# Splitting 24 weight tiles during the first feed-forward, and token-major last down products, in a hybrid decoder layer

## The chip, the cores and the metric

The kernel runs on one core of one Trainium2 chip. The metric is the time of one execution on the device, in microseconds, median of several runs. The engines named below are PE (TensorE, matrix products; PEld is its weight load), DVE (VectorE), ACT (ScalarE), POOL (GpSimd) and SP (SyncE, which here only issues DMAs).

## The reference, cut to what matters

One decoder layer over 1032 tokens: a prompt of 1024 and 8 sample tokens that each have a paged cache of 2048. All arrays are fp32, the model width is 1024, the feed-forward width 2816.

```python
def swiglu(x, wg, wu, wd):
    return (jax.nn.silu(x @ wg) * (x @ wu)) @ wd
...
h = layer_norm(ALPHA * x + 0.5 * swiglu(x, ffn1_wg, ffn1_wu, ffn1_wd), ln1_g, ln1_b)
q_a, k_a, v_a, q_i, k_i, w_i, q_r, k_r, v_r, g_r = jnp.split(h @ w_in, _split_points(), axis=-1)
o_a = attend(q_a, k_a, v_a, q_i, k_i, w_i)   # indexer scores, top-k keys per query, softmax over them
o_r, s_new = retention(qr, kr, vr, s0)       # 4 heads of 128, chunkwise, with rotary q and k
mix = jnp.concatenate([o_a.reshape(B, S, W_A), y_r], axis=-1) @ w_out
h = layer_norm(ALPHA * h + mix, ln2_g, ln2_b)
h = layer_norm(ALPHA * h + 0.5 * swiglu(h, ffn2_wg, ffn2_wu, ffn2_wd), ln3_g, ln3_b)
```

Outputs are the last h for prompt and sample, the new keys, values and indexer keys, and the retention states.

## The kernel before, in words

**Tiling and precision.** Activations lie feature-major: 128 features on the partitions, tokens along the row, in three chunks of 344 tokens (CW). Each fp32 product is made of three matmuls (`mm3`, lines 169 to 171): an operand is split into a high part (a rounded copy) and a low part (the remainder), and high by high, high by low and low by high are added up in PSUM. A weight tile is 128 x 1024, 512 KB.

**Stages.** First feed-forward (0 to about 745 us): chunk 0 by plain products, then chunks 1 and 2 together (`chunks12`) by products of a seven-product scheme, over eleven pairs p of feed-forward tiles; the down products of pairs 9 and 10 come last (`last`). Then the first layer norm, the projections with `w_in` (chunk-wise products named pw_qi, pw_kr and so on), indexer scores (around 800 to 890), the top-k search beside the retention heads (890 to 1110), ties, attention (1150 to 1340), the output projection with `w_out` (1340 to 1470), the sample tokens' attention, and the second feed-forward (about 1520 to 2290). At its end the output's layer norm (`ln_out`) follows on the last down products.

**The weight tiles of the middle.** `Weights` holds a list of tiles in the order of use. `w_raw` has SP load one tile into a single raw buffer (line 142); `w_split` has ACT cast it to the high part (line 152) and GpSimd subtract for the low part (line 154), into one of two pairs of buffers. While one pair is in use by a product, the next tile is split into the other pair as soon as its last reader is done, and the next raw load follows. The list is: three indexer query tiles (qi1 to qi3), gr0, then kr, vr, qr and gr of heads 1 to 3, then the twelve tiles va, qa and ka of attention, then the eight tiles wo of the output projection, and ten more.

**Order.** The program is written as generators that a scheduler (`g.s`) steps by a modelled time: a `yield` of so many microseconds or `tick` moves it. The order in which instructions stand on each engine follows from that, and each engine works its own list in order. The feed-forward's weights stream through a free list of slots (`g.fs`); `Stream.keep` is the number of slots that the stream leaves free.

**The tail.** `f2.last(c, after)` makes, for each of 8 output tiles o of 128 features, 12 matmuls of 344 tokens (weights stationary, lines 403 to 405), then VectorE adds the result to z (line 407). `ln_out` makes for each tile of 128, 128 or 88 tokens eight transposes back to token-major (line 710), statistics (lines 713 and 716), the reciprocal root (lines 633 to 638), two scalings and additions per half of 512 features (line 720, then 722 on ACT and 723 on GpSimd, or 725 on VectorE), and an output DMA (lines 727 and 729).

## Time and profile before

| | us |
|---|---|
| median of 3 runs | 2312.18 |
| lowest and highest run | 2311.66, 2313.08 |
| the profiled execution | 2311.91 |
| its span in the trace | 2310.1 |

The profiled execution is one run; its span is the time from the first to the last instruction that the trace holds. A row of a timeline reads: start, duration, engine, line, operation, output<-inputs, shapes, and in brackets the idle time before it with what ended it. "The chain of waits" is followed back from the last instruction, at each step to what released it. Names of tiles are those of the program: wr_ is a raw weight tile, wh_ and wl_ its high and low parts, pw_ a projection's PSUM tile, zt the small tables of the search.

### The profile page before, as it was taken

The page shows a single profiled execution, that of the slowest core. Times are in us where ns is not written, and L with a number is a line of the kernel's source. Part 1 is how long each engine was busy: PE and PEld are TensorE (multiplying, and loading weights), DVE is VectorE, ACT ScalarE, POOL GpSimd, SP SyncE. Part 2 cuts the span into 40 slices and gives each one's busy share as a digit, 9 for nine tenths or more (in the row PEclk, how much of TensorE's full clock was granted, in tenths as well). Part 3 has the DMA queues.
Part 4 walks back from the last instruction along what each step waited for, and adds up shares of the span by engine and source line. Part 5 has one row for each costly group of instructions (what it writes and reads, how often), then busy time and mean ns, then how long its engine had stood idle before and what let it go on. Part 6 is the DMA issues. An engine that isn't in the chain of part 4 may idle for free.

```text
span 2310.1 us, 36886 instructions
## 1 busy us (share of the span) xinstructions
PE 2220.8 (96%) x14155; PEld 2144.3 (93%) x14155; DVE 1761.8 (76%) x3745; ACT 1072.4 (46%) x1931; POOL 323.4 (14%) x342
## 2 busy tenths in 40 slices
PE   8999999999999999889899999889999999999996
PEld 8999999999999989778789989879799999999996
DVE  5655797887878578678966678988568789887866
ACT  5433343332334465878466665343435444333331
POOL 0000100000002303444122234313210000000002
PEclk9999999999999999999999999989999999999998
DMA  8544332222222211121332142336544332222211
GB/s 266 156 136 146 109 89 74 83 75 64 82 75 97 93 25 46 53 69 49 88 89 56 51 141 80 121 123 189 177 129 137 98 103 80 92 73 65 92 65 49
DMA packets 239182, 224.32 MB, mean 97 GB/s; under 512 B 13098, under 2 KB 219774, under 8 KB 238238
## 3 DMA queue, kind: packets, MB, share of 16 engines
q1 hardware_dynamic: 235166, 209.38, 30.0%
q0 software_dynamic: 3840, 12.59, 1.7%
q8 instruction: 111, 1.82, 0.3%
q14 instruction: 65, 0.53, 0.1%
HBM read 200.91 MB, written 22.59 MB: 97 GB/s over the span
## 4 chain that ended last, share of the span: by engine, by line
PE 78%; DVE 11%; ACT 6%; issue 3%; DMA 1%; POOL 0%; POOLq 0%; SPq 0%; DVEq 0%; ACTq 0%
PE pds_f L403 5%; PE pds_f L404 5%; PE pds_f L405 5%; PE pg_f L169 2%; PE pu_f L169 2%; PE pg_f L170 2%; PE pg_f L171 2%; PE pdp_f L403 2%; PE pu_f L171 2%; PE pu_f L170 2%; PE pdp_f L404 2%; PE pdp_f L405 2%; ACT ja L1034 2%; PE ps_f1U L169 2%; PE ps_f2G L170 2%
## 5 line engine op out<-in xcount | busy, mean ns | idle before, releaser
L407 DVE SCALAR_TENSOR_TENSOR z<-pds_f,z 128x344 f32<-128x344 f32 x320 | 164.6, 516 | 125.9 <-PE pds_f L405 124.7
L403 PE MATMUL pds_f<-gs_f,wh_f1ds 128*128 128x344 f32 x352 | 114.1, 325 | 0.1
L407 DVE SCALAR_TENSOR_TENSOR z<-pdp_f,z 128x344 f32<-128x344 f32 x160 | 80.0, 512 | 44.1 <-PE pdp_f L405 43.9
L403 PE MATMUL pds_f<-gs_f,wh_f2ds 128*128 128x344 f32 x352 | 113.4, 322 | 0.0
L405 PE MATMUL pds_f<-gs_f,wl_f1ds 128*128 128x344 f32 x352 | 113.2, 322 | 0.0
L404 PE MATMUL pds_f<-gs_f,wh_f1ds 128*128 128x344 f32 x352 | 113.1, 321 | 0.0
L405 PE MATMUL pds_f<-gs_f,wl_f2ds 128*128 128x344 f32 x352 | 112.4, 319 | 0.0
L404 PE MATMUL pds_f<-gs_f,wh_f2ds 128*128 128x344 f32 x352 | 112.4, 319 | 0.0
L1034 ACT ACTIVATE ja<-key,zt 128x1024 bf16<-128x1024 int16 (+5 forms) x90 | 93.7, 1041 | 34.6 <-DVE zt L1045 33.1
L723 POOL TENSOR_TENSOR yt<-yt,ln_b_rows 128x512 f32<-128x512 f32 (+1 forms) x9 | 12.0, 1352 | 570.3 <-ACT yt L722 570.3
L296 ACT CAST wS_f1G<-ws_f1G 128x512 fp32r<-128x512 f32 x44 | 25.0, 618 | 133.5 <-PE pds_f L404 68.1
L1508 ACT CAST p<-pT 128x512 fp32r<-128x512 f32 (+2 forms) x112 | 47.4, 433 | 54.1 <-PE pT L1504 41.9
L296 ACT CAST wS_f2G<-ws_f2G 128x512 fp32r<-128x512 f32 x44 | 25.7, 619 | 93.4 <-PE pds_f L405 80.7
L403 PEld LDWEIGHTS pds_f<-gs_f,wh_f1ds 128*128 128x128 f32 x352 | 66.8, 190 | 1.1 <-DVE z L407 0.3
L404 PEld LDWEIGHTS pds_f<-gs_f,wh_f1ds 128*128 128x128 f32 x352 | 66.7, 190 | 0.2
L405 PEld LDWEIGHTS pds_f<-gs_f,wl_f1ds 128*128 128x128 f32 x352 | 66.7, 189 | 0.0
L403 PEld LDWEIGHTS pds_f<-gs_f,wh_f2ds 128*128 128x128 f32 x352 | 66.2, 188 | 0.2 <-ACT gs_f L465 0.2
L404 PEld LDWEIGHTS pds_f<-gs_f,wh_f2ds 128*128 128x128 f32 x352 | 66.2, 188 | 0.0
L405 PEld LDWEIGHTS pds_f<-gs_f,wl_f2ds 128*128 128x128 f32 x352 | 66.1, 188 | 0.0
L612 POOL TENSOR_TENSOR lns_l<-z 128x344 f32<-128x344 f32 x3 | 2.8, 929 | 442.2 <-DVE z L407 428.0
L1509 DVE TENSOR_TENSOR p<-pT,p 128x512 fp32r<-128x512 f32 (+2 forms) x112 | 54.5, 497 | 8.7 <-ACT p L1508 7.5
L1470 ACT ACTIVATE z<-z,mn 128x896 f32<-128x896 f32 (+3 forms) x64 | 49.8, 778 | 20.0 <-DVE mn L1467 15.7
(815 smaller groups left out, 8651.0 us busy)
## 6 DMA issues: line engine op xcount, KB each, us to landing
wr_f1g<-in_ffn_wg_dram SPq DMA_DIRECT2D x22, 512.0 KB
wr_f1u<-in_ffn_wu_dram SPq DMA_DIRECT2D x22, 512.0 KB
wr_f1dp<-in_ffn_wd_dram SPq DMA_DIRECT2D x22, 512.0 KB
wr_f1G<-in_ffn_wg_dram SPq DMA_DIRECT2D x22, 512.0 KB
wr_f1U<-in_ffn_wu_dram SPq DMA_DIRECT2D x22, 512.0 KB
wr_f1ds<-in_ffn_wd_dram SPq DMA_DIRECT2D x22, 512.0 KB
wr_f2u<-in_ffn_wu_dram SPq DMA_DIRECT2D x22, 512.0 KB
wr_f2g<-in_ffn_wg_dram SPq DMA_DIRECT2D x22, 512.0 KB
```

The source lines that it names most:

```text
L169: g.nc.tensor.matmul(ps, w[0][:, k, :], x[0][:, k, :], start=first and i == 0, stop=False)
L170: g.nc.tensor.matmul(ps, w[0][:, k, :], x[1][:, k, :], start=False, stop=False)
L171: g.nc.tensor.matmul(ps, w[1][:, k, :], x[0][:, k, :], start=False, stop=last and i == n - 1)
L296: nc.scalar.copy(t[:, 0], src)
L403: g.nc.tensor.matmul(ps, wh[:, o, :], th, start=i == 0, stop=False)
L404: g.nc.tensor.matmul(ps, wh[:, o, :], tl, start=False, stop=False)
L405: g.nc.tensor.matmul(ps, wl[:, o, :], th, start=False, stop=i == len(grp) - 1)
L407: g.nc.vector.scalar_tensor_tensor(out=z, in0=ps, scalar=0.5 / ALPHA, in1=z, op0=OP.mult, op1=OP.add)
L1034: nc.scalar.activation(jk[:, 0:n], key[b], AF.Sign, bias=t[:, j:j + 1], scale=-1.0, accum_out=cnt[:, j:j + 1])
L1470: nc.scalar.activation(z[:, 0:n], z[:, 0:n], AF.Exp, bias=prev, scale=-1.0, accum_out=mn[:, 3:4])
L1508: nc.scalar.copy(ph[:, js, ts], ptv[:, js, ts])
L1509: nc.vector.tensor_tensor(out=pl[:, js, ts], in0=ptv[:, js, ts], in1=ph[:, js, ts].bitcast(F32), op=OP.subtract)
```

## The change

It has two parts.

**A.** A new generator, `presplit`, runs beside `chunks12` of the first feed-forward from its second pair (p of 1) on. It takes three slots of the feed-forward's free list. For each of 24 tiles (qi1 to qi3, gr0, the twelve tiles of heads 1 to 3, and the eight wo) GpSimd issues a DMA that loads the raw tile, ACT casts it, VectorE subtracts, and GpSimd issues two DMAs that write both parts to a scratch array in device memory (`wscr`). Later `Weights.split` has SP load both parts from there into the pair of buffers. The tiles va, qa, ka and the last ten are treated as before. `chunks12` is called with `tight` at 11 in place of 0, so the weight stream leaves 4 slots free, not 1, in the gate's products of every pair.

**B.** For the last chunk of the last feed-forward's last down products, `last_tok` takes the place of `last`. For each tile of tokens and each half of the features, four matmuls against twice ALPHA times the identity put z token-major into a PSUM bank, and 12 matmuls with 512 columns of the weights as the moving operand add the down products. `ln_out` then reads that bank: it makes no transposes for this chunk, and VectorE makes no addition to z. Its epsilon is scaled to match. Output DMAs of the very last tile are issued per half.

The first place is GpSimd's list in the search, at head 1's query rotation (swq, qT) and the split of the next key tile (wl_kr is the low part of kr2). Before:

```order
L1115 TENSOR_TENSOR swq_2_9353<-swq_2_9353,sin 128x344
L1116 TENSOR_TENSOR qT_9173<-qT_9173,swq_2_9353 128x344
L154 TENSOR_TENSOR wl_kr_9429<-wr_kr_9223,wh_kr_9427 128x1024
L1118 COPY zt_7756<-qT_9173 128x8
L1145 TENSOR_TENSOR qd_9377<-qT_9173,ic 128x1024
L1587 DMA kgs<-in_cache_kidx_dram,s1sm 128x512
```

The same place now:

```order
L1138 TENSOR_TENSOR swq_2_9528<-swq_2_9528,sin 128x344
L1139 TENSOR_TENSOR qT_9350<-qT_9350,swq_2_9528 128x344
L1141 COPY zt_7949<-qT_9350 128x8
L1168 TENSOR_TENSOR qd_9552<-qT_9350,ic 128x1024
L1610 DMA kgs<-in_cache_kidx_dram,s1sm 128x512
```

The subtraction of 128x1024 is gone between the rotation and the copy; the operations around it stand as before.

The second place is SP's list of DMAs in the search, where the weights of head 1 are loaded (mscr and s1sm are small tables). Before:

```order
L142 DMA wr_kr_8562<-in_w_in_dram 128x8x128
L142 DMA wr_vr_8774<-in_w_in_dram 128x8x128
L142 DMA wr_qr_9002<-in_w_in_dram 128x8x128
L1563 DMA s1sm<-in_e_dram 8x256
L1218 DMA mscr<-gT_8725 128x1024
L142 DMA wr_gr_9110<-in_w_in_dram 128x8x128
```

Now:

```order
L1976 DMA w_kr_8953<-wscr 128x1024
L1976 DMA w_kr_8954<-wscr 128x1024
L1976 DMA w_vr_9179<-wscr 128x1024
L1976 DMA w_vr_9180<-wscr 128x1024
L1241 DMA mscr<-gT_8908 128x1024
L1586 DMA s1sm<-in_e_dram 8x256
L1976 DMA w_qr_9285<-wscr 128x1024
L1976 DMA w_qr_9286<-wscr 128x1024
L1976 DMA w_gr_9396<-wscr 128x1024
L1976 DMA w_gr_9397<-wscr 128x1024
```

Each raw load of a tile has become two loads from the scratch array, one for each part, and the store to mscr has moved ahead of the third tile's loads.

The third place is the end of TensorE's list (pds_f is a bank of down products, yp one of transposes, tm a token-major bank, gs_f the gated activations). Before, the last output tile and chunk 2's transposes of its second half:

```order
L403 MATMUL pds_f_2_7_23706<-gs_f_23273,wh_f2ds_23175 128x344
L404 MATMUL pds_f_2_7_23706<-gs_f_23274,wh_f2ds_23175 128x344
L405 MATMUL pds_f_2_7_23706<-gs_f_23273,wl_f2ds_23176 128x344
L403 MATMUL pds_f_2_7_23706<-gs_f_23274,wh_f2ds_23194 128x344
L404 MATMUL pds_f_2_7_23706<-gs_f_23275,wh_f2ds_23194 128x344
L405 MATMUL pds_f_2_7_23706<-gs_f_23274,wl_f2ds_23195 128x344
L710 MATMUL yp_1_23720<-ident,z_15602 128x128 x3
L710 MATMUL yp_1_23726<-ident,z_15602 128x128 x3
L710 MATMUL yp_1_23720<-ident,z_15602 128x128
L710 MATMUL yp_1_23726<-ident,z_15602 128x128
L710 MATMUL yp_1_23732<-ident,z_15602 88x128 x4
```

Now, the last of six such groups:

```order
L545 MATMUL tm_256_1_23857<-ident_23536,z_15747 88x128 x4
L551 MATMUL tm_256_1_23857<-wh_f2ds_23280,gs_f_23135 88x512
L552 MATMUL tm_256_1_23857<-wl_f2ds_23281,gs_f_23135 88x512
L553 MATMUL tm_256_1_23857<-wh_f2ds_23280,gs_f_23136 88x512
L551 MATMUL tm_256_1_23857<-wh_f2ds_23301,gs_f_23136 88x512
L552 MATMUL tm_256_1_23857<-wl_f2ds_23302,gs_f_23136 88x512
```

Transposes of all three tiles stood behind the last down product; now a tile's four identity products and twelve weight products follow each other, tile by tile and half by half.

The diff:

```diff
--- before.py
+++ after.py
@@ -537,6 +537,22 @@
         for o in range(8):
             self.down('s', grp, c, {f: tiles[(f, c)] for f in grp}, o, after)
+    def last_tok(self, c, t, n, q, ident):
+        g, mm = self.g, self.g.nc.tensor.matmul
+        ps = bank(g, 'tm', f"tm{c}_{t}_{q}")
+        for j in range(4):
+            mm(ps[0:n, 128 * j:128 * j + 128], self.z[c][:, 4 * q + j, t:t + n], ident, start=j == 0, stop=False)
+        grp = self.pairs[9] + self.pairs[10]
+        tiles = {**self.gt[9][0], **self.gt[10][0]}
+        for i, f in enumerate(grp):
+            th, tl = (v[:, t:t + n] for v in tiles[(f, c)])
+            wh, wl = (v[:, 4 * q:4 * q + 4, :].rearrange("p k f -> p (k f)") for v in self.st.want(f"{self.tag}ds{f}")[0:2])
+            mm(ps[0:n, :], th, wh, start=False, stop=False)
+            mm(ps[0:n, :], th, wl, start=False, stop=False)
+            mm(ps[0:n, :], tl, wh, start=False, stop=i == len(grp) - 1)
+        return ps
 def halves_of(t):
     return t[:, 0:4, :], t[:, 4:8, :]
@@ -692,29 +708,35 @@
         done()
-def ln_out(g, z, t0, t, n, prog, slot, gb, o, lag=(0.0, 0.0)):
+def ln_out(g, z, t0, t, n, prog, slot, gb, o, lag=(0.0, 0.0), tok=None):
     nc = g.nc
     V = nc.vector
     pt = []
+    epsv, epst = (EPS / ALPHA ** 2, g.eps_ln) if tok is None else (4 * EPS, g.eps_tok)
     for q in range(2):
-        while prog[0] < 4 * q + 4:
+        while prog[0] < 4 * q + 4 if tok is None else len(tok) <= q:
             yield 0.25
         if lag[q]:
             yield lag[q]
         if q == 0:
             mem = g.ms.tile([P, 16], F32, tag="lot", name=f"lot{t0}", bufs=3)
             st, mv = mem[:, 0:12].rearrange("p (a b) -> p a b", a=2), mem[:, 12:16]
-        p = bank4(g, 'aux', f"yp{t0}_{q}")
-        for j in range(4):
-            nc.tensor.transpose(p[0:n, j, :], z[:, 4 * q + j, t:t + n], g.ident)
-        g.s.t += 0.4
-        pt.append(p[0:n].rearrange("p a b -> p (a b)"))
+        if tok is not None:
+            pt.append(tok[q][0:n])
+        else:
+            p = bank4(g, 'aux', f"yp{t0}_{q}")
+            for j in range(4):
+                nc.tensor.transpose(p[0:n, j, :], z[:, 4 * q + j, t:t + n], g.ident)
+            g.s.t += 0.4
+            pt.append(p[0:n].rearrange("p a b -> p (a b)"))
         V.bn_stats(out=st[0:n, q, :], in_=pt[q])
         yield 0.1
     y = A(g, slot, f"yt{t0}", F32, D)
     V.bn_aggr(out=mv[0:n, 0:2], in_=st[0:n])
-    rsqrt(g, mv[0:n, 2:3], mv[0:n, 1:2], g.eps_ln, EPS / ALPHA ** 2, mv[0:n, 3:4])
+    rsqrt(g, mv[0:n, 2:3], mv[0:n, 1:2], epst, epsv, mv[0:n, 3:4])
+    m = min(n, 1024 - t0)
     for q in range(2):
         sl = slice(512 * q, 512 * q + 512)
         V.scalar_tensor_tensor(out=y[0:n, sl], in0=pt[q], scalar=mv[0:n, 0:1], in1=gb['ln3_g'][0:n, sl], op0=OP.subtract, op1=OP.mult)
@@ -723,10 +745,11 @@
             nc.gpsimd.tensor_tensor(out=y[0:n, sl], in0=y[0:n, sl], in1=gb['ln3_b'][0:n, sl], op=OP.add)
         else:
             V.scalar_tensor_tensor(out=y[0:n, sl], in0=y[0:n, sl], scalar=mv[0:n, 2:3], in1=gb['ln3_b'][0:n, sl], op0=OP.mult, op1=OP.add)
-    m = min(n, 1024 - t0)
-    nc.sync.dma_start(o['y_prompt'][0, t0:t0 + m, :], y[0:m])
-    if m < n:
-        nc.sync.dma_start(o['y_sample'].rearrange("b s d -> (b s) d"), y[m:n])
+        if m < n:
+            nc.sync.dma_start(o['y_prompt'][0, t0:t0 + m, sl], y[0:m, sl])
+            nc.sync.dma_start(o['y_sample'].rearrange("b s d -> (b s) d")[:, sl], y[m:n, sl])
+    if m == n:
+        nc.sync.dma_start(o['y_prompt'][0, t0:t0 + m, :], y[0:m])
 def load_x(g, xp, xs, x, B, z):
@@ -1900,23 +1923,60 @@
     nc.sync.dma_start(ascr[:, :, 1024:1032].rearrange("h p b -> p h b"), on)
+def presplit(g, tiles, wscr, made):
+    nc = g.nc
+    while g.plain or len(g.fs) < 5:
+        yield 0.5
+    own = [g.fs.get() for _ in range(3)]
+    def fetch(n):
+        raw = A8(g, own[0], f"pr_{tiles[n][1]}")
+        nc.gpsimd.dma_start(raw, tiles[n][0])
+        return raw
+    raw = fetch(0)
+    yield 8.0
+    for n, (src, name) in enumerate(tiles):
+        hi, lo = A8(g, own[1], f"ph_{name}", F32R), A8(g, own[2], f"pl_{name}", F32R)
+        nc.scalar.copy(hi, raw)
+        nc.vector.tensor_tensor(out=lo, in0=raw, in1=hi.bitcast(F32), op=OP.subtract)
+        yield 2.0
+        if n + 1 < len(tiles):
+            raw = fetch(n + 1)
+        for j, t in enumerate((hi, lo)):
+            nc.gpsimd.dma_start(wscr[n, j], t.rearrange("p k f -> p (k f)").bitcast(F32))
+        made[name] = (wscr[n, 0], wscr[n, 1])
+        yield 13.5
+    g.fs.put(*own)
 class Weights:
-    def __init__(self, g, tiles, split=True):
-        self.g, self.tiles = g, tiles
+    def __init__(self, g, tiles, split=True, made={}):
+        self.g, self.tiles, self.made = g, tiles, made
         self.raw, self.ready = [], None
         self.fetch()
         if split:
             self.split()
     def fetch(self):
-        while self.tiles and len(self.raw) < len(self.g.raws):
+        while self.tiles and self.tiles[0][1] not in self.made and len(self.raw) < len(self.g.raws):
             self.raw.append(w_raw(self.g, *self.tiles.pop(0)))
     def split(self):
-        if self.raw:
-            self.ready = w_split(self.g, self.raw.pop(0))
+        g = self.g
+        if not self.raw and self.tiles and self.tiles[0][1] in self.made:
+            name = self.tiles.pop(0)[1]
+            pair = g.pairs[g.pi % len(g.pairs)]
+            g.pi += 1
+            self.ready = tuple(A8(g, q, f"w{j}_{name}", F32R) for j, q in enumerate(pair))
+            for t, src in zip(self.ready, self.made[name]):
+                g.nc.sync.dma_start(t.rearrange("p k f -> p (k f)").bitcast(F32), src)
+            self.fetch()
+        elif self.raw:
+            self.ready = w_split(g, self.raw.pop(0))
             self.fetch()
     def get(self):
@@ -2041,11 +2101,21 @@
     def ready(p, i):
         need = {2: 'T2', 3: 'T1', 4: 'T3', 6: 'T4'}.get(i)
         s.until(lambda: need is None or need in B)
+        g.plain = p < 1
+    tiles = [(wcols(w_in, 1536 + 128 * ct), f"qi{ct}") for ct in (1, 2, 3)] + [(wcols(w_in, 3656), "gr0")]
+    for hd in (1, 2, 3):
+        tiles += [(wcols(w_in, c0 + 128 * hd), f"{n}{hd}") for c0, n in ((2632, "kr"), (3144, "vr"), (2120, "qr"), (3656, "gr"))]
+    tiles += [(wcols(w_out, 128 * oo), f"wo{oo}") for oo in range(8)]
+    made = {}
+    g.plain = True
+    ahead = s.add(presplit(g, list(tiles), dp.tile([len(tiles), 2, P, 1024], F32, name="wscr"), made))
     f1.chunk0(x[0], hook, parked)
     psum['out'] = True
     setbanks(g, ch=[0, 1, 2, 3], dn=[4, 5], aux=[6, 7])
-    f1.chunks12(B, ready)
+    f1.chunks12(B, ready, 11)
+    s.drain(ahead)
     S_.close("msF")
@@ -2171,18 +2241,13 @@
                 rX['qr0'] = w_raw(g, wcols(w_in, colX['qr0']), 'qr0')
-    tiles = [(wcols(w_in, 1536 + 128 * ct), f"qi{ct}") for ct in (1, 2, 3)] + [(wcols(w_in, 3656), "gr0")]
-    for hd in (1, 2, 3):
-        tiles += [(wcols(w_in, c0 + 128 * hd), f"{n}{hd}") for c0, n in ((2632, "kr"), (3144, "vr"), (2120, "qr"), (3656, "gr"))]
-    for ct in range(4):
-        tiles += [(wcols(w_in, c0 + 128 * ct), f"{n}{ct}") for c0, n in ((1024, "va"), (0, "qa"), (512, "ka"))]
     rows = [(w_out[128 * k:128 * k + 128, :].rearrange("p (k f) -> p k f", k=8), f"wr{k}") for k in (2, 3)]
     halves = [[(w_out[r:r + 512, 256 * j:256 * j + 256].rearrange("(k p) (h f) -> p k h f", p=P, h=2), f"wh{r}_{j}") for j in range(4)] for r in (0, 512)]
-    tiles += [(wcols(w_out, 128 * oo), f"wo{oo}") for oo in range(8)] + rows + halves[1]
+    tiles = tiles[:16] + [t for ct in range(4) for t in ((wcols(w_in, 1024 + 128 * ct), f"va{ct}"), (wcols(w_in, 128 * ct), f"qa{ct}"), (wcols(w_in, 512 + 128 * ct), f"ka{ct}"))] + tiles[16:] + rows + halves[1]
     g.raws, g.ri, g.pairs, g.pi = [0], 0, PAIRS[:2], 0
     g.lo_eng = [nc.gpsimd]
     g.mixlo = [nc.vector]
-    wq = Weights(g, tiles)
+    wq = Weights(g, tiles, True, made)
     def tile(evac, name, pace=0.0):
         w = wq.get()
@@ -2524,14 +2589,27 @@
     outs = []
     gb = rows()
-    setbanks(g, dn=[0, 1, 2], aux=[3, 4, 5, 6, 7])
-    for c in (1, 2):
-        prog = [0]
-        put_out(c, gb, prog, 4, 0.0, ((0.0, 2.5), (1.5, 0.0))[c - 1])
-        def after(o):
-            prog[0] = o + 1
-        f2.last(c, after)
+    setbanks(g, dn=[0, 1], aux=[2, 3, 4, 5, 6, 7], tm=[0, 1, 2, 3, 4, 5])
+    ident2 = g.ms.tile([P, 128], F32, name="ident2")
+    nc.scalar.mul(ident2, g.ident, 2 * ALPHA)
+    g.eps_tok = g.ms.tile([P, 1], F32, name="eps_tok")
+    nc.vector.memset(g.eps_tok, 4 * EPS)
+    prog = [0]
+    put_out(1, gb, prog, 4, 0.0, (0.0, 2.5))
+    def after(o):
+        prog[0] = o + 1
+    f2.last(1, after)
+    for j, t in enumerate(range(0, CW, 128)):
+        tok = []
+        if j:
+            s.until(lambda: not s.live(outs[j - 1]))
+        n = min(128, CW - t)
+        outs.append(s.add(ln_out(g, None, 2 * CW + t, t, n, None, own['y'][(3 + j) % 4], gb, o, (0.0, 0.0), tok)))
+        for q in range(2):
+            tok.append(f2.last_tok(2, t, n, q, ident2))
+            s.tick(3.7)
     s.drain(*outs)
     S_.close("msP", "ap", "ps", "xp", "dp", "cp")
```

## The prediction, made before the changed kernel was run

> **What bounds the kernel now.** I read the page first (busy shares, then the chain by engine), then a table of busy time by stretch, then the chain of waits inside the stretches where the 24 tiles are used, and last the timelines of the tail. Times are from one execution of 2311.91 us with a span of 2310.1 us; the median of the runs is 2312.18 us, 0.27 us more.
>
> ```profile
> span 2310.1 us, 36886 instructions
> PE 2220.8 (96%) x14155; PEld 2144.3 (93%) x14155; DVE 1761.8 (76%) x3745; ACT 1072.4 (46%) x1931; POOL 323.4 (14%) x342
> PE 78%; DVE 11%; ACT 6%; issue 3%; DMA 1%; POOL 0%; POOLq 0%; SPq 0%; DVEq 0%; ACTq 0%
> GB/s 266 156 136 146 109 89 74 83 75 64 82 75 97 93 25 46 53 69 49 88 89 56 51 141 80 121 123 189 177 129 137 98 103 80 92 73 65 92 65 49
> ```
>
> TensorE is busy for 2220.8 of 2310.1 us, so all the idle time that any edit could win back is about 89 us, and the 17% of the chain that lies on DVE and ACT says where it is. The next table's columns are the stretch, its length, then busy us (and instructions) of PE, PEld, DVE, ACT and POOL, the granted clock, the DMA share and GB/s.
>
> ```profile
> 350.00:400.00 50.00, 50.00 (x319) 49.90 (x318) 40.63 (x75) 17.07 (x31) 0.00 (x0) 1.00 0.25 74
> 800.00:890.00 90.00, 86.42 (x521) 80.03 (x520) 70.01 (x150) 57.11 (x107) 14.05 (x8) 0.98 0.11 28
> 890.00:1110.00 220.00, 198.18 (x1347) 185.11 (x1346) 173.64 (x474) 168.63 (x334) 99.58 (x113) 0.95 0.22 60
> 1340.00:1470.00 130.00, 120.58 (x822) 113.53 (x821) 107.34 (x395) 73.62 (x158) 42.57 (x49) 0.99 0.38 119
> 1900.00:1950.00 50.00, 50.00 (x322) 49.90 (x321) 48.95 (x96) 27.73 (x45) 0.00 (x0) 1.00 0.33 102
> ```
>
> The feed-forwards (first and last rows) keep TensorE full. Where the 24 tiles are used, TensorE idles for 3.6 us (800 to 890), 21.8 us (890 to 1110, the top-k search beside the retention heads) and 9.4 us (1340 to 1470, the output projection): 34.8 us in all.
>
> **Part A, what it removes: the splits beside the search.** Each of the 24 tiles loses one cast on ACT and one subtraction on GpSimd. The subtraction costs more than GpSimd's time:
>
> ```profile
> 943.20 2.37 POOL L154 TENSOR_TENSOR wl_kr<-wr_kr,wh_kr 128x1024 fp32r<-128x1024 f32 x1
> ```
> ```profile
> 943.29 2.30 DVE L1044 TENSOR_TENSOR zt<-zt 128x6 f32<-128x6 f32 x1 [1.48 <-ACT ja L1034]
> ```
> ```profile
> L1044 DVE TENSOR_TENSOR zt<-zt x32: 119/166/2359, 920.5 to 1107.1; 128x6 f32<-128x6 f32 x32
> ```
>
> The same VectorE operation on 6 columns takes 0.166 us at the median and 2.30 us when a GpSimd subtraction starts just before it; both end at 945.6 us. VectorE stood still for that subtraction. The Trainium skill (SBUF — State Buffer, "Who interferes with whom") calls the port pair that VectorE and GpSimd share an exclusive lock; the trace agrees, 2.30 against 0.166 us.
>
> Which of these stalls are on the path is read from the chain of waits of 890 to 1110 us (start, us, what):
>
> ```profile
> 894.28 2.01 DVE zt L982
> 911.33 2.44 issue
> 929.53 0.95 ACT wh_gr L152
> 941.28 1.04 ACT wh_kr L152
> 943.29 2.31 DVE zt L1044
> 961.22 0.52 ACT wh_vr L152
> 986.86 2.31 DVE zt L626
> 1020.21 1.05 ACT wh_kr L152
> 1022.39 2.11 issue
> 1062.97 0.95 ACT wh_qr L152
> 1065.79 2.41 DVE zt L627
> 1082.92 2.08 DVE s1sm L1639
> ```
>
> Four DVE pieces (943.29, 986.86, 1065.79, 1082.92) are tiny operations that should take about 0.17 us, like the median of L1044: 2.31 + 2.31 + 2.41 + 2.08 less 4 x 0.17 is 8.4 us. The piece at 894.28 is a larger operation; I leave it 0.5 us and count 1.5. The two "issue" pieces (2.44 and 2.11) fall on two more subtractions, and I count 3.5 of their 4.55 us. The five casts are 0.95 + 1.04 + 0.52 + 1.05 + 0.95 = 4.5 us. Together 17.9 us. In the output projection the chain of 1340 to 1470 us has
>
> ```profile
> 1364.70 1.05 ACT wh_wo L152
> 1416.48 2.25 DVE zt L1680
> ```
>
> that is 1.05 + 2.08 = 3.1 us by the same subtraction. So at most 17.9 + 3.1, **21 us**, can go, against the 34.8 us that TensorE idles there. Less will: in 890 to 1110 us TensorE is 90% busy and ACT 77%, and the chain changes engine every microsecond or so, so the next chain is close behind. When a stall goes, the next thing late is a projection's matmul or the search's own pass on ACT (L1034). I have no row for the second-longest chain. The ends are 0 (each stall is replaced) and 21 us; I take a little over the middle, **12 us**, because subtractions and casts off this chain go too.
>
> **Part A, what it puts in their place.** SP now loads two halves per tile in place of one raw tile, straight into the pair of buffers that the product reads. Before, the raw tile came early into its own buffer, and only cast and subtraction stood between a freed pair and the product. Now the whole load does, on a queue where it stands behind whatever SP waits for. The DMA rates of 780 to 830 us, in 40 slices of 1.25 us, hold two raw tiles:
>
> ```profile
> GB/s 0 0 0 0 0 0 0 33 324 62 0 13 5 195 220 0 0 0 6 228 186 0 5 204 0 0 0 0 7 13 0 0 7 0 0 0 0 0 0 52
> ```
> ```profile
> L154 POOL TENSOR_TENSOR wl_kr<-wr_kr,wh_kr x3: 2367/2382/2398, 873.8 to 1022.2; 128x1024 fp32r<-128x1024 f32 x3
> L154 POOL TENSOR_TENSOR wl_wo<-wr_wo,wh_wo x8: 2377/2392/2401, 1345.5 to 1438.3; 128x1024 fp32r<-128x1024 f32 x8
> L152 ACT CAST wh_kr<-wr_kr x4: 1045/1048/1051, 699.2 to 1020.2; 128x1024 fp32r<-128x1024 f32 x4
> ```
>
> The first burst is 1.25 us x (33 + 324 + 62) GB/s = 0.52 MB, one tile in under 3.75 us, so a pair of 1 MB needs 5 to 7.5 us, against 1.05 + 2.39 = 3.4 us for the split. With two pairs, a load has the time that the other pair's tile is in use. From the second head's key tile to the fourth's there are 8 tiles in 1022.2 - 873.8 = 148.4 us, 18.6 us each; among the output tiles 92.8 / 7 = 13.3 us. So the load hides, by 6 us at the tightest, and I cost it at 0; if the cover went it would be the excess over 13.3 us, eight times.
>
> **Part A, the first feed-forward.** 24 x 1.05 = 25 us of casts on ACT, and 24 subtractions on VectorE:
>
> ```profile
> L154 DVE TENSOR_TENSOR wl_kr<-wr_kr,wh_kr x1: 1215/1215/1215, 739.4 to 739.4; 128x1024 fp32r<-128x1024 f32 x1
> ```
>
> 24 x 1.215 = 29 us, over some 400 us: VectorE goes from 40.63 of 50 us (81%) to about 88%. The second feed-forward ran VectorE at 48.95 of 50 us (98%) beside a TensorE at 50.00 of 50, so the work hides, and TensorE, being full, can neither gain. The traffic is 24 x 1.5 MB = 38 MB in 400 us, 94 GB/s on top of 74; the first slice of the page moved 266 GB/s. The three slots taken leave the weight stream fewer; the second feed-forward ran with such a tighter store in its first pairs. I take **0**, with 29 us (all VectorE's time laid on TensorE) as the far end. A direct load of 0.5 MB issued by GpSimd has no row. The nearest, its gathers, have the answer
>
> ```profile
> DMA to landing us min/median/max: 3.6/4.0/4.3
> ```
>
> and SP's loads take under 3.75 us. The program lays about 13.5 us between a tile's fetch and its cast. I take 5 us, with 0 and 13.5 as ends, none on the path.
>
> **Part B, the tail.** The rows that carry it:
>
> ```profile
> 723.44 0.88 PE L678 MATMUL pr_l<-ident,lnm_l 128*128 128x128 f32 x6
> 724.07 0.40 PE L405 MATMUL pds_f<-gs_f,wl_f1ds 128*128 128x344 f32 x1
> ...
> 807.63 0.39 PE L974 MATMUL sc<-kl,qst 128*128 128x512 f32 x1
> 807.86 0.37 PE L973 MATMUL sc<-kst,qst 128*128 128x448 f32 x1
> ...
> 2272.63 0.49 PE L710 MATMUL yp<-ident,z 128*128 128x128 f32 x3
> ...
> 2290.78 1.21 PE L710 MATMUL yp<-ident,z 128*128 128x128 f32 x8
> ```
> ```profile
> 2304.01 1.26 POOL L723 TENSOR_TENSOR yt<-yt,ln_b_rows 88x512 f32<-88x512 f32 x1 [1.46 <-ACT yt L722]
> ```
> ```profile
> 2305.67 0.32 SPq L729 DMA_DIRECT2D out_y_sample_dram<-yt  x1
> ```
>
> A matmul that moves 512 columns takes 0.23 us to the next (807.63 to 807.86), an fp32 one of 128 columns 0.63 / 3 = 0.21. From 2272.63, where chunk 1's last down product ends, TensorE now does chunk 1's 12 transposes (8 take 1.21, so 1.8 us) and six groups of 4 x 0.21 + 12 x 0.23 = 3.6 us: 21.6 us, to **2296.0 us**, 5.2 us later than the down products ended before (2290.78). But two of the three tiles are then through. Before, three tiles came at once, and from 2290.78 to the end of the last addition (2304.01 + 1.26 = 2305.27) 14.5 us passed. Now one remains: a third of that is 4.8 us, and I add 0.6 because a single tile has no neighbour to fill its handovers, to 2301.4. Four output DMAs in place of two, 0.32 us each, put the last issue at 2302.4 to 2303, and the 4.43 us that lay between the last issue and the end (2310.1 - 2305.67) give 2306.8 to 2307.4. I take the later, **-2.7 us**; the ends are +1.6 (the last tile takes 4.3 us more, two thirds of a second tile) and -5 (it takes 2.3 us less, half of its third).
>
> The **sum** on the profiled execution: 2311.91 - 12 - 2.7 + 0 = 2297.2, with the 0.27 us to the median **2297.5 us**.
>
> **The rivals.**
>
> *The stalls are replaced.* The search and the projections are two chains of nearly one length, the second keeps the time, and only the tail's 2.7 us are left: 2309.5 us. For it speaks TensorE's 90% in 890 to 1110; against it that the retention's own small VectorE operations (L626, L627) are stalled too, so both chains get shorter. 0.11.
>
> *All of it converts.* 21 + 2.7 us: 2288.5 us. The 34.8 us of idle TensorE allow it. 0.18.
>
> *Slower: the loads that GpSimd issues come late in the feed-forward.* The cast stands in ACT's order; if its raw tile hasn't landed, ACT waits, and the first feed-forward's gates (ACT's and VectorE's products) wait behind it, until TensorE has no operand. It decides from a landing of 13.5 us on; each microsecond beyond costs up to 24. It is slower than before once 24 x excess is over 14.7 us, 0.6 us each; with 1.5 us each it gives 2297.5 + 36 = 2333.5 us. For it speaks that VectorE is near 88% there; against it the 3.6 to 4.3 us of the gathers. 0.07. A rule of the Trainium skill speaks for it: by SBUF — State Buffer, "SBUF: two separate sides", GpSimd can't write the descriptors of its own DMAs while VectorE runs an operation that takes both ports, and such DMAs belong on SP's or ACT's queue. No row of this trace shows a direct GpSimd DMA beside such an operation; the gathers, which landed in at most 4.3 us, don't.
>
> *The tail doesn't do what it says.* If the weights as moving operand ran at half the rate, 72 x 0.23 = 16.6 us would be added: 2314 us. Only row 807.63 speaks to it, against. 0.03.
>
> **How the numbers follow.** The forecast with its neighbours (6 to 19 us gained) has 0.61; with the full conversion 0.18 the change is faster by over 0.2% (4.6 us, about what a measurement of this kernel can tell from no change) with 0.79. Within 0.2%: the replaced stalls and most of the slow tail, 0.13. Slower: 0.08. The range of 2285 to 2310 us reaches from just below the full conversion with a tail of -5 us (2312.2 - 21 - 5 = 2286.2) to the replaced stalls, and leaves out the slower cases and a little of each side.
>
> **What would show it.** In the changed profile, 300 to 700 us should still hold TensorE at 50.00 of 50 us, with VectorE at 44 to 45. The 2-us pieces on 6- and 8-column operations should be gone from the chain between 850 and 1085 us, and remain where other GpSimd operations run. TensorE's idle time in the search should shrink by 8 to 10 us, and by 2 to 3 in the output projection. The tail's last matmul should end about 2296 us less what was won before, with one tile's work after it. Wrong would be: ACT waiting for a raw tile in the feed-forward, TensorE waiting for a weight pair's DMA, or a search that lasts as long with other things on its chain.

## The result, and the profile after

The changed kernel takes 2338.09 us (median of 4 runs, 2334.84 to 2339.01) against 2312.3 us before: a ratio of 1.0107, 95% interval 1.0095 to 1.0119. It is **slower by 1.1%**, outside the stated range. The profiled execution took 2334.84 us; its page begins and its chain by engine reads

```profile
span 2332.9 us, 37102 instructions
PE 2231.0 (96%) x14155; PEld 2149.1 (92%) x14155; DVE 1753.1 (75%) x3762; ACT 1072.3 (46%) x1932; POOL 314.2 (13%) x390
PE 53%; DVE 12%; ACT 7%; DMA 5%; issue 3%; POOL 1%; POOLq 0%; DVEq 0%; ACTq 0%; SPq 0%
```

The span grew by 22.8 us and TensorE's busy time by 10; "DMA", 1% of the chain before, is now 5%. Where it came from is read by the start of the same instruction in both traces:

| what starts | before, us | after, us | difference |
|---|---|---|---|
| first feed-forward's first down product of chunks 1, 2 | 311.2 | 312.0 | +0.8 |
| its last down matmul | 740.5 | 787.3 | **+46.8** |
| search, last pass on ACT | 1106.0 | 1117.4 | +11.4 |
| attention (first key transpose) | 1173.2 | 1203.1 | +29.9 |
| second feed-forward | 1522.1 | 1548.2 | +26.1 |
| behind chunk 1's last down product | 2272.63 | 2298.11 | +25.5 |
| end of span | 2310.1 | 2332.9 | +22.8 |

So the first feed-forward lost 46 us, the middle won 46.8 - 25.5 = 21.3, and the tail 2.7. The stretches of busy time (length, then PE, PEld, DVE, ACT, POOL, clock, DMA share, GB/s) of the changed kernel

```profile
320.00:670.00 350.00, 320.26 (x1958) 314.60 (x1957) 265.04 (x475) 126.62 (x211) 44.61 (x68) 0.98 0.54 166
350.00:400.00 50.00, 46.38 (x292) 45.53 (x291) 38.70 (x70) 19.24 (x33) 5.93 (x9) 1.00 0.53 168
1900.00:1950.00 50.00, 50.00 (x324) 49.86 (x323) 45.88 (x95) 24.68 (x40) 0.00 (x0) 1.00 0.32 103
```

and the same 350 us of the kernel before

```profile
320.00:670.00 350.00, 350.00 (x2223) 349.59 (x2222) 284.64 (x523) 122.95 (x218) 0.00 (x0) 1.00 0.25 74
```

say that TensorE lost 30 of 350 us there, and that VectorE wasn't the cause by its load: it did less in that time, not more. The list of waits of 320 to 670 us (who, for whom, us in all, times, longest) has what is new (rows between these are left out):

```profile
ACT ph_wo L1942 <- DMA pr_wo<-in_w_out_dram: 45.8, 7, 9.3
...
ACT ph_qr L1942 <- DMA pr_qr<-in_w_in_dram: 22.9, 3, 8.2
ACT ph_gr L1942 <- DMA pr_gr<-in_w_in_dram: 20.0, 4, 8.4
ACT ph_vr L1942 <- DMA pr_vr<-in_w_in_dram: 18.7, 3, 9.1
ACT ph_kr L1942 <- DMA pr_kr<-in_w_in_dram: 13.5, 3, 5.4
ACT ph_qi L1942 <- DMA pr_qi<-in_w_in_dram: 13.4, 2, 7.2
...
PEld pds_f L403 <- DVE z L407: 19.5, 13, 2.7
PE pds_f L403 <- DVE z L407: 15.9, 11, 2.4
PE ps_f1G L169 <- DVE pc_f1U L469: 13.1, 6, 4.1
PEld ps_f1G L169 <- ACT wh_f1ds L273: 11.7, 5, 4.3
```

ACT waited 134 us in all for the raw tiles of its casts (first six rows). TensorE (PE and PEld) waits for VectorE's additions and for ACT's casts of the weight stream; in the kernel before, the same list has no wait of TensorE at all. One cycle, on GpSimd, ACT, VectorE and TensorE:

```profile
410.35 0.91 POOL L1935 DMA_DIRECT2D pr_gr<-in_w_in_dram  x1 [27.27 <-DVE pl_qr L1943]
411.25 0.55 POOL L1948 DMA_DIRECT2D wscr<-pl_qr  x1
...
418.59 0.91 POOL L1935 DMA_DIRECT2D pr_kr<-in_w_in_dram  x1 [0.92 <-DVE pl_gr L1943]
```
```profile
415.80 1.05 ACT L1942 CAST ph_gr<-pr_gr 128x1024 fp32r<-128x1024 f32 x1 [8.40 <-DMA pr_gr<-in_w_in_dram]
...
423.86 1.05 ACT L1942 CAST ph_kr<-pr_kr 128x1024 fp32r<-128x1024 f32 x1 [5.43 <-DMA pr_kr<-in_w_in_dram]
```
```profile
408.84 1.22 DVE L1943 TENSOR_TENSOR pl_qr<-pr_qr,ph_qr 128x1024 fp32r<-128x1024 f32 x1
...
417.07 1.23 DVE L1943 TENSOR_TENSOR pl_gr<-pr_gr,ph_gr 128x1024 fp32r<-128x1024 f32 x1 [1.82 <-DMA wscr<-pl_qr]
418.21 0.93 DVE L407 SCALAR_TENSOR_TENSOR z<-pds_f,z 128x344 f32<-128x344 f32 x2
```
```profile
418.78 0.43 PE L403 MATMUL pds_f<-gs_f,wh_f1ds 128*128 128x344 f32 x1 [1.40 <-DVE z L407]
```

A raw load (410.35) is issued only when the subtraction before it (408.84) has freed the one raw buffer; its tile lands 5.4 us later; and the cast that wants it has been standing at the head of ACT's list for 8.4 us. VectorE then stands still for 1.8 us. The row names the store of the previous low half, which ended last; but the cast itself ends only at 415.80 + 1.05 = 416.85 us, so the store adds 0.2 us at most. The addition to z (418.21) stands behind that subtraction, and TensorE waits for it. A cycle takes 417.07 - 408.84 = 8.2 us. The instruction list of ACT (not a profile) shows how casts come to stand like that; these are the two casts that ran at 462.71 and 470.76 us:

```
L461 ACTIVATE pc_f1G_4287<-pc_f1G_4287 128x344
L1942 CAST ph_qr_5062<-pr_qr_4902 128x1024
L1942 CAST ph_gr_5268<-pr_gr_5114 128x1024
L296 CAST wS_f1U_4593<-ws_f1U_4336 128x512
```

Two casts stand next to each other, the weight stream's casts behind them. The program's yields place them 15.5 us apart; the order that comes out at build doesn't keep that.

The middle and the tail went as hoped or better. Between the two feed-forwards the rows are, before and after (columns as above),

```profile
740.50:1522.10 781.60, 723.39 (x4782) 675.90 (x4780) 601.84 (x1709) 479.70 (x992) 242.36 (x268) 0.98 0.26 77
```
```profile
787.30:1548.20 760.90, 715.69 (x4782) 672.97 (x4780) 578.81 (x1709) 457.30 (x968) 186.19 (x244) 0.98 0.31 95
```

With the same 4782 matmuls, TensorE's idle time falls from 58.2 to 45.2 us and its busy time by 7.7 us. The operation on 6 columns that took up to 2359 ns (search, L1044 before, L1067 now) reads

```profile
L1067 DVE TENSOR_TENSOR zt<-zt x32: 149/166/781, 958.1 to 1118.4; 128x6 f32<-128x6 f32 x32
```

and the tail, on TensorE and SP,

```profile
2298.11 0.49 PE L731 MATMUL yp<-ident,z 128*128 128x128 f32 x3
...
2299.73 0.40 PE L552 MATMUL tm<-wl_f2ds,gs_f 128*128 128x512 f32 x1
2299.96 0.40 PE L553 MATMUL tm<-wh_f2ds,gs_f 128*128 128x512 f32 x1
...
2321.24 0.40 PE L553 MATMUL tm<-wh_f2ds,gs_f 128*88 128x512 f32 x1
```
```profile
2327.35 0.66 SPq L750 DMA_DIRECT2D out_y_sample_dram<-yt  x2
```

Its matmuls stand 0.23 us apart, and from 2298.11 to the last one's start pass 23.1 us.

### The profile page after: what moved, and what is told of

The parts are those of the page before. It is cut to its first block, busy times and chain, and to the rows that moved or that the text cites. A ratio compares the mean times of both kernels' runs of the same rounds, so it can differ in the third digit from the quotient of the medians.

```text
span 2332.9 us, 37102 instructions
## 1 busy us (share of the span) xinstructions
PE 2231.0 (96%) x14155; PEld 2149.1 (92%) x14155; DVE 1753.1 (75%) x3762; ACT 1072.3 (46%) x1932; POOL 314.2 (13%) x390
## 4 chain that ended last, share of the span: by engine, by line
PE 53%; DVE 12%; ACT 7%; DMA 5%; issue 3%; POOL 1%; POOLq 0%; DVEq 0%; ACTq 0%; SPq 0%
ACT ja L1057 3%; PE pds_f L403 3%; PE pds_f L404 3%; PE pds_f L405 3%; PE ps_f2U L170 2%; PE ps_f2G L170 2%; PE ps_f2G L169 2%; PE ps_f2U L171 2%; PE ps_f2G L171 2%; PE ps_f2U L169 2%; PE pg_f L169 1%; PE pg_f L170 1%; PE pg_f L171 1%; PE pu_f L169 1%; DMA wscr<-pl_wo 1%
## 5 line engine op out<-in xcount | busy, mean ns | idle before, releaser
L407 DVE SCALAR_TENSOR_TENSOR z<-pds_f,z 128x344 f32<-128x344 f32 x312 | 157.8, 513 | 109.4 <-PE pds_f L405 108.6
L403 PE MATMUL pds_f<-gs_f,wh_f2ds 128*128 128x344 f32 x320 | 102.6, 321 | 0.0
L404 PE MATMUL pds_f<-gs_f,wh_f2ds 128*128 128x344 f32 x320 | 102.2, 320 | 0.0
L405 PE MATMUL pds_f<-gs_f,wl_f2ds 128*128 128x344 f32 x320 | 102.2, 320 | 0.0
L745 POOL TENSOR_TENSOR yt<-yt,ln_b_rows 128x512 f32<-128x512 f32 (+1 forms) x9 | 11.4, 1287 | 567.2 <-ACT yt L744 567.2
L1531 ACT CAST p<-pT 128x512 fp32r<-128x512 f32 (+2 forms) x112 | 47.5, 433 | 58.3 <-PE pT L1527 45.2
L403 PEld LDWEIGHTS pds_f<-gs_f,wh_f2ds 128*128 128x128 f32 x320 | 60.1, 188 | 0.3 <-ACT gs_f L465 0.2
L404 PEld LDWEIGHTS pds_f<-gs_f,wh_f2ds 128*128 128x128 f32 x320 | 60.2, 188 | 0.0
L405 PEld LDWEIGHTS pds_f<-gs_f,wl_f2ds 128*128 128x128 f32 x320 | 60.1, 188 | 0.0
L169 PE MATMUL pg_f<-xh,wh_f1g 128*128 128x344 f32 x176 | 57.5, 326 | 2.8 <-ACT xh L785 2.8
L169 PE MATMUL pg_f<-h2h,wh_f2g 128*128 128x344 f32 x176 | 58.8, 334 | 0.0
```

The lines of the kernel that those rows point to most:

```text
L169: g.nc.tensor.matmul(ps, w[0][:, k, :], x[0][:, k, :], start=first and i == 0, stop=False)
L403: g.nc.tensor.matmul(ps, wh[:, o, :], th, start=i == 0, stop=False)
L404: g.nc.tensor.matmul(ps, wh[:, o, :], tl, start=False, stop=False)
L405: g.nc.tensor.matmul(ps, wl[:, o, :], th, start=False, stop=i == len(grp) - 1)
L407: g.nc.vector.scalar_tensor_tensor(out=z, in0=ps, scalar=0.5 / ALPHA, in1=z, op0=OP.mult, op1=OP.add)
L1531: nc.scalar.copy(ph[:, js, ts], ptv[:, js, ts])
```

## The experiments

The measure is the start of the first feed-forward's last down matmul (740.5 us before, 787.3 after), and the total against the kernel before on the same chip, whose median lay between 2312.9 and 2313.9 us.

**One part at a time.** First the tighter weight stream alone, in the kernel before:

```diff
-    f1.chunks12(B, ready)
+    f1.chunks12(B, ready, 11)
```

> The kernel before, with only the weight stream of the first feed-forward held tighter (4 slots left free in all eleven pairs, as in the change). Four theories for the 46.8 us by which the first feed-forward's last down matmul starts later (740.5 us before, 787.3 after). Cycle: a tile's cast waits in ACT's order for a raw load that is issued only when the previous tile's subtraction is done, the subtraction waits in VectorE's order for the previous store, and TensorE waits behind both. Load: the casts and subtractions themselves are too much beside a full TensorE. Traffic: the 38 MB slow the stream's own weight loads. Slots: the tighter stream and the three slots taken. Here cycle, load and traffic expect 740 to 742 us for that matmul and 2312 us in all; slots expects up to 787 and up to 2359 us.

Measured: 744.5 us; 2315.61 us (ratio 1.0008, 0.9998 to 1.0019). Then casts and subtractions alone (in the four runs that do a part of the work, `made` isn't given to `Weights`, which splits the tiles as before):

```diff
-        if n + 1 < len(tiles):
-            raw = fetch(n + 1)
-        for j, t in enumerate((hi, lo)):
-            nc.gpsimd.dma_start(wscr[n, j], ...)
+        if n + 1 == len(tiles):
+            for j, t in enumerate((hi, lo)):
+                nc.gpsimd.dma_start(wscr[n, j], ...)
```

> The changed kernel with the 24 casts and 24 subtractions left in the first feed-forward, but all of them on one raw tile that is loaded once, and only the last result is stored; the 24 tiles are then split in the middle as before (so what was stored isn't used). Cycle and traffic expect the last down matmul of the first feed-forward at 741 to 746 us and 2310 to 2315 us in all (the tail keeps its 2.5 us); load expects it near 787 and 2356 us in all.

Measured: 746.5 us; 2315.74 us (1.0010, 0.9999 to 1.0020). And the DMAs alone:

```diff
-        nc.scalar.copy(hi, raw)
-        nc.vector.tensor_tensor(out=lo, in0=raw, in1=hi.bitcast(F32), op=OP.subtract)
-        for j, t in enumerate((hi, lo)):
-            nc.gpsimd.dma_start(wscr[n, j], t...)
+        for j in range(2):
+            nc.gpsimd.dma_start(wscr[n, j], raw...)
```

> The changed kernel with the 24 raw loads and 48 stores left (the raw tile is stored twice), but without the casts and subtractions; the 24 tiles are split in the middle as before. Three slots are taken, two of them used. Cycle and load expect the last down matmul of the first feed-forward at 740 to 746 us and 2310 to 2315 us in all; traffic expects it near 787 us and 2356 us in all, as does slots.

Measured: 743.3 us; 2315.79 us (1.0009, 0.9999 to 1.0020). The rows of 320 to 670 us are, of the run with compute alone and of that with DMAs alone,

```profile
320.00:670.00 350.00, 350.00 (x2217) 348.75 (x2216) 302.51 (x542) 141.62 (x237) 1.11 (x2) 1.00 0.25 77
```
```profile
320.00:670.00 350.00, 350.00 (x2221) 349.20 (x2220) 282.63 (x521) 122.14 (x218) 43.79 (x66) 1.00 0.53 175
```

TensorE stays full in both, with VectorE at 302.51 of 350 us in the one and twice the traffic in the other. All three totals, and two of the three matmuls, came out up to 4 us above what the theories without a loss here had expected, so none of the parts is quite free. But as the cause of the 46.8 us load, traffic and slots fall: 3 to 6 us each.

**Halves of tiles**, two of each in the same three slots, as a first remedy:

```diff
+    for m in range(2 * len(tiles)):
...
+        raw, hi, lo = (t[:, 4 * b:4 * b + 4, :] for t in (R, H, L))
...
+        yield 6.75
```

> The changed kernel with the same three slots, cut in halves: each tile is loaded, cast, subtracted and stored in two halves of 512 columns, so that one half loads while the other is split (48 loads, casts and subtractions, 96 stores). Cycle expects the 46.8 us to shrink to 5 to 25: last down matmul at 745 to 765 us, 2293 to 2313 us in all. Load, traffic and slots expect no less than the change's 787 us and 2335 to 2345 us, since there are more instructions and DMAs.

Measured: 786.9 us; 2332.54 us (1.0083, 1.0066 to 1.0100). The theory of the cycle, as I had put it, was wrong in this: cutting the tiles doesn't shorten it by what I expected, because a half's cast still stands right behind its load: ACT waited 104 us in all for halves that were still on their way.

**Which coupling.** Without the stores:

```diff
-        for j, t in enumerate((hi, lo)):
-            nc.gpsimd.dma_start(wscr[n, j], ...)
+        if n + 1 == len(tiles):
+            for j, t in enumerate((hi, lo)):
+                nc.gpsimd.dma_start(wscr[n, j], ...)
```

> The changed kernel with raw loads, casts and subtractions in the first feed-forward, but without the stores (only the last tile's), and with the 24 tiles split in the middle as before. Before this run: the tighter stream alone, casts and subtractions alone, and DMAs alone each moved the last down matmul of the first feed-forward by only 3 to 6 us (743 to 746 us), where the change has 787. So the loss is in what couples them. Coupled raw load: a cast waits on ACT for a load that is issued behind the previous subtraction. It expects most of the loss to stay here, a cycle of about 6.5 us instead of 8.2 for each of three tiles of a pair: last down matmul at 760 to 780 us, 2330 to 2350 us in all. Coupled store: a subtraction waits on VectorE for the previous low half's store. It expects 743 to 750 us here, 2312 to 2318 us in all.

Measured: 768.3 us; 2338.77 us (1.0109, 1.0089 to 1.0129), as the coupled raw load expected, with ACT waiting up to 8.5 us for a load:

```profile
ACT ph_wo L1942 <- DMA pr_wo<-in_w_out_dram: 33.2, 7, 6.7
...
ACT ph_kr L1942 <- DMA pr_kr<-in_w_in_dram: 16.2, 3, 8.5
```

Without the raw loads, but with the stores:

```diff
-        if n + 1 < len(tiles):
-            raw = fetch(n + 1)
```

> The changed kernel with casts, subtractions and all 48 stores in the first feed-forward, but with one raw tile that is loaded once; the 24 tiles are split in the middle as before. Coupled store expects most of the loss to stay: last down matmul at 770 to 787 us, 2338 to 2356 us in all. Coupled raw load expects a small rest, 745 to 755 us and 2313 to 2325 us in all.

Measured: 749.8 us; 2327.03 us (1.0058, 1.0038 to 1.0078). The feed-forward came out as the raw-load theory said; the total is 2 us over its range, and 5 us of it arose between the two feed-forwards, as they did in the run with DMAs alone; I haven't explained them. So the run with raw loads loses 27.8 of the 46.8 us and the run with stores 9.3 (casts and subtractions, which both have, cost 6.0 alone), and the two together cost more than their sum.

**The low half in place of the raw tile**, so that two slots alternate as raw tiles:

```diff
+        raw = A8(g, own[n % 2], f"pr_{tiles[n][1]}")
...
+        hi, lo = A8(g, own[2], f"ph_{name}", F32R), raw.bitcast(F32R)
```

> The whole change with the same three slots used otherwise: the subtraction writes the low half in place of the raw tile, so two slots alternate as raw tiles and the next raw tile is loaded while this one is split; no subtraction waits for a store. Both coupling theories expect most of the 47 us to go: last down matmul at 743 to 755 us and, with the 24 us won behind it, 2290 to 2302 us in all. If instead the sum of tighter stream, engine work and traffic is what costs (3.8 + 6 + 2.6 us alone, more together), it stays at 780 to 790 us and 2333 to 2340 us.

Measured: 762.5 us; 2311.56 us (0.9991, 0.9981 to 1.0000). Half of the loss is gone, not most: casts still waited 74 us in all for raw tiles (320 to 720 us). **The tail alone**, that is the change without part A:

```diff
-    ahead = s.add(presplit(...))
...
-    f1.chunks12(B, ready, 11)
-    s.drain(ahead)
+    f1.chunks12(B, ready)
```

> The kernel before with the token-major last down products alone (no split in the first feed-forward, no tighter stream). From the changed kernel's trace the tail gave 2.6 us: 2309 to 2311 us in all. If the tail's gain hung on the other part, 2312 to 2314.

Measured: 2309.56 us (0.9983, 0.9973 to 0.9992): it stands by itself.

**Holding the loads back.** A mark (`g.mark`) is set in the chains, and a one-column copy from the marked product precedes the load:

```diff
+        nc.gpsimd.tensor_copy(raws[n][:, 0, 0:1], g.mark[0:P, 0:1])
         nc.gpsimd.dma_start(raws[n], tiles[n][0])
...
                 nc.scalar.copy(q[1], ps)
+                g.mark = q[1]
```

> The change with its 16 first tiles only (the eight tiles of the output projection are split in the middle as before), the low half in place of the raw tile, and each raw load held back by a one-column copy on GpSimd that reads the gate product of the current chain, one tile in each gate chain and one in each up chain. The instruction lists then no longer bunch three tiles behind each other. Bunching theory (the lists put three tiles of a pair into one stretch of down products, where three cycles of 8.2 us don't fit): the first feed-forward's last down matmul at 744 to 750 us (tighter stream and engine work remain), 2296 to 2304 us in all (17 us of the middle and 2.6 of the tail won, the output projection's 3.7 not). If the coupling costs wherever it stands: 755 to 775 us, 2308 to 2325 us in all.

> The same for all 24 tiles, three in each pair: at the start of the gate chain, at its end, and at the start of the up chain. Bunching theory: last down matmul at 745 to 754 us, 2293 to 2303 us in all. If three tiles in a pair are too many wherever they stand: 760 to 787 us, 2310 to 2335 us in all.

> The change's own three buffers (one raw tile, one high and one low half), all 24 tiles, but each raw load held back to its place like in the run before, so that a cast stands about 14 us behind its load. Bunching theory: nearly all of the 47 us goes although the buffers are as in the change: last down matmul at 745 to 756 us, 2293 to 2305 us in all. Buffer theory (the single raw tile and the store before the next subtraction are what cost): 775 to 790 us, 2325 to 2340 us in all.

Measured: 768.1, 776.0 and 777.1 us; 2324.96, 2327.15 and 2327.55 us (1.0046, 1.0032 to 1.0060; 1.0058, 1.0044 to 1.0072; 1.0064, 1.0050 to 1.0078). **This bunching theory fell:** three casts no longer stood together (in the second of the three runs they start 9 to 20 us apart), and most of the loss stayed. The third run came out in the range of the buffer theory, which is so far as good as any. The timelines of GpSimd and ACT in the second of the three runs say why:

```profile
542.00 0.91 POOL L1939 DMA_DIRECT2D pr_gr<-in_w_in_dram  x1 [0.35 <-POOL pr_gr L1938]
```
```profile
546.56 1.05 ACT L1948 CAST ph_gr<-pr_gr 128x1024 fp32r<-128x1024 f32 x1 [5.16 <-DMA pr_gr<-in_w_in_dram]
```

The load had been moved back, and the cast had been placed up to it again: ACT reached it at 541.4 and waited 5.16 us. Each of this run's 24 casts starts 4.5 to 7.0 us after its load was issued, and in the change 4.8 to 6.8: in both a cast runs when its tile lands. So what counts may be not how the tiles are spread but how far a cast stands behind its own load, and the next runs try that.

**Holding the casts back** instead, by the same copy into the cast's output:

```diff
-        nc.gpsimd.tensor_copy(raws[n][:, 0, 0:1], g.mark[0:P, 0:1])
...
+            nc.gpsimd.tensor_copy(hi[:, 0, 0:1], g.mark[0:P, 0:1])
             nc.scalar.copy(hi, raw)
```

> All 24 tiles, low half in place of the raw tile, three tiles in each pair; held back is now the cast, not the load: GpSimd first copies one column of the current chain's product into the high half's buffer, so the cast can't stand in ACT's list ahead of the next mark, while its raw tile was loaded from one mark before. In the run with the loads held back, each cast stood right behind its load again and ACT waited up to 6 us for it. In-order theory (the loss is ACT and VectorE waiting in their order for a tile that is still being loaded): last down matmul of the first feed-forward at 746 to 756 us, 2294 to 2304 us in all, and no wait of a cast on a load over 1 us. If the combined work of engines, copies and traffic is what costs: 765 to 780 us, 2315 to 2330 us.

> The same with the 16 first tiles only, two in each pair. In-order theory: last down matmul at 744 to 752 us, 2295 to 2303 us in all. Combined work: 760 to 770 us, 2315 to 2325 us.

Measured: 743.8 and 741.4 us; 2291.76 us (0.9905, 0.9890 to 0.9920) and 2298.62 us (0.9936, 0.9922 to 0.9949), within the in-order theory's ranges or up to 3 us below them. Neither run lists a wait of a cast for a load (300 to 720 us). With the change's own buffers:

```diff
-        raws[n] = A8(g, own[n % 2], f"pr_{tiles[n][1]}")
+        raws[n] = A8(g, own[0], f"pr_{tiles[n][1]}")
...
-            hi, lo = A8(g, own[2], f"ph_{name}", F32R), raw.bitcast(F32R)
+            hi, lo = A8(g, own[1], f"ph_{name}", F32R), A8(g, own[2], f"pl_{name}", F32R)
```

> All 24 tiles with the change's own three buffers (one raw tile, one high and one low half) and the casts held back as in the run at 2291.8 us, three in each pair. In-order theory: the buffers matter little once no cast stands right behind its load: last down matmul of the first feed-forward at 744 to 754 us, 2291 to 2303 us in all. Buffer theory (the low half written in place made the difference): 760 to 787 us, 2308 to 2335 us.

Measured: 744.0 us; 2291.38 us (0.9904, 0.9887 to 0.9920). Of this run, the row of 320 to 670 us, then GpSimd and ACT, then all its waits of a cast for a load in these 350 us:

```profile
320.00:670.00 350.00, 348.63 (x2210) 347.70 (x2210) 304.80 (x545) 145.21 (x243) 53.59 (x95) 1.00 0.58 180
```
```profile
443.14 0.92 POOL L1938 DMA_DIRECT2D pr_vr<-in_w_in_dram  x1 [0.93 <-DVE pl_kr L1949]
...
456.57 0.21 POOL L1947 CAST ph_vr<-pc_f1U 128x1 fp32r<-128x1 f32 x1 [11.98 <-ACT pc_f1U L478]
```
```profile
440.33 1.05 ACT L1948 CAST ph_kr<-pr_kr 128x1024 fp32r<-128x1024 f32 x1 [0.51 <-DMA pr_kr<-in_w_in_dram]
...
456.92 1.05 ACT L1948 CAST ph_vr<-pr_vr 128x1024 fp32r<-128x1024 f32 x1
```
```profile
ACT ph_wo L1948 <- DMA pr_wo<-in_w_out_dram: 1.8, 1, 1.8
...
ACT ph_kr L1948 <- DMA pr_kr<-in_w_in_dram: 0.5, 1, 0.5
```

The same 24 tiles, instructions, buffers and traffic as in the change, plus 24 copies of one column. This cast now stands 13.8 us behind its load (443.14 to 456.92). Of all 24, sixteen stand 12 us or more behind and eight 5.5 to 7.7 us. ACT waits 2.3 us in all for loads, where it waited 134, and the loss of 46.8 us is 3.5. Against the third run with the loads held back, one line has moved: the copy stands before the cast and not before the load. There ACT waited 76 us in all for loads, and the matmul started at 777.1 us. With this the buffer theory falls too: own buffers and the low half in place differ by 0.2 us (744.0 and 743.8).

**The lock in the middle.** In the kernel before, one word:

```diff
-    g.lo_eng = [nc.gpsimd]
+    g.lo_eng = [nc.vector]
```

> The kernel before with one word changed: the subtractions of the middle's weight tiles run on VectorE (1.2 us) instead of GpSimd (2.4 us, VectorE standing still for it). It asks how much of the 20 us that the change wins in the middle is the lock. If the lock is most of it: 2300 to 2308 us, since half of each stall goes. If it is the casts, the loads and the shorter path from a freed pair to the next tile: 2310 to 2316 us.

Measured: 2300.26 us (0.9944, 0.9928 to 0.9961). In the search, the 6-column operation and a weight tile's subtraction now read

```profile
L1044 DVE TENSOR_TENSOR zt<-zt x32: 132/166/2026, 915.0 to 1099.5; 128x6 f32<-128x6 f32 x32
```
```profile
L154 DVE TENSOR_TENSOR wl_kr<-wr_kr,wh_kr x4: 1215/1224/1948, 740.2 to 1008.1; 128x1024 fp32r<-128x1024 f32 x4
```

VectorE does the work itself in half the time for which it stood still. The time is in the range of the lock; but the edit also shortens each subtraction from 2.39 to 1.22 us, and what that is worth by itself isn't separated. The same line changed in the last run with casts held back:

> The run with 24 tiles, the change's own buffers and the casts held back (2291.4 us), and with the subtractions of the remaining weight tiles of the middle (twelve for attention and ten behind them) on VectorE instead of GpSimd. If each of these subtractions still stops VectorE on the path: 2282 to 2289 us. If attention, where TensorE was busy for 185 of 190 us, hides them: 2289 to 2293 us.

In this run only the twelve subtractions of va, qa and ka move: the ten behind them ran on VectorE already, in the kernel before too. Measured: 2284.78 us (0.9876, 0.9860 to 0.9893), 1.2% faster than the kernel before and 2.3% faster than the change.

## Why the prediction was wrong, point by point

- **The step that failed** is "The program lays about 13.5 us between a tile's fetch and its cast", and with it "I take 5 us, with 0 and 13.5 as ends, none on the path" and the cost of 0 for the first feed-forward. The landing was sized rightly: 5.2 to 6.3 us in the changed kernel. The 13.5 us were taken from the program's yields. In the lists as built, the load stood behind the previous subtraction and the cast right behind the load: every cast started 4.8 to 6.8 us after its load's issue, as the tile landed, and ACT waited 134 us in all. With the casts held back, the same step costs 3.5 us: the 0 was nearly right for the order that it assumed. The prediction had named the sign itself, "ACT waiting for a raw tile in the feed-forward".
- The cover named for that step was "the work hides, and TensorE, being full, can neither gain". As to load this holds from 320 to 670 us: compute alone left TensorE at 350.00 of 350 us, though the end of the feed-forward moved by 6.0 us, 4.0 of which the tighter stream costs alone. A wait in an in-order list is no load, and a busy share can't show it.
- The rival "the loads that GpSimd issues come late in the feed-forward" had the mechanism (a cast in ACT's order waits, the gates behind it) and the sign, but a wrong point: it was to decide from a landing of 13.5 us on. It gave 2333.5 us at a chance of 0.07; measured was 2338. A rule of the Trainium skill stood beside it (SBUF — State Buffer, "SBUF: two separate sides": while VectorE runs an operation in a two-port mode, GpSimd can't write the descriptors of its own DMAs). The traces don't bear it out as the cause: the change's raw loads landed in 5.2 to 6.3 us, without the casts and subtractions in 4.4 to 7.9, and with them but without the stores in 4.6 to 4.7.
- The middle was mis-sized: 12 us forecast, 21.3 measured (787.3 to 2298.11 against 740.5 to 2272.63), as much as the 21 us I gave as the end. TensorE's idle time between the feed-forwards fell by 13.0 us, close to the forecast. The other 7.7 us are busy time of the same matmuls, for which the sum had no term; most of it lies before attention (399.01 us before, 392.22 after, at a granted clock of 0.97 and 0.98). The mechanism held as far as the 2.3-us stalls on the search's 6-column operation are gone; beside a subtraction that the change leaves, such a stall remains (2.25 us at 1119.60). How the 21.3 us divide among stalls, casts and loads is open: moving all 36 subtractions of the middle to VectorE, with casts and loads as before, is worth 12.8 us (2313.08 to 2300.26), but 12 of them belong to the tiles that the change leaves, and moving these alone gave 6.6 us (2291.38 to 2284.78). About 6 us are then left for the 24 tiles, an estimate from these two differences. The search itself won 35 us (from +46.8 to +11.4) and gave 18.5 back before attention. There, from 1120 to 1150 us, VectorE is busy for 29.04 of 30 us, among other things with the search's ties, and TensorE then waits 5.7 and 4.8 us for operations of the last head that stand in VectorE's list. What would shorten this wasn't tried.
- The loads of 1 MB that take the place of a split cost nothing that the trace shows: from 787 to 1548 us no wait of any engine for them is listed. No experiment took them apart.
- The tail was right: -2.7 us forecast, 2.7 measured (34.8 us from chunk 1's last down product to the end, 37.5 before), with the last matmul ending 23.5 us behind that point against 23.4 forecast, and 0.17% faster alone.
